# The triangular inverse of an RWKV block done in two halves of the heads instead of all at once

## The chip, the cores and the metric

The kernel runs on one core of a Trainium2 chip. The metric is the device time of one execution in microseconds (us), lower is better. The engines are PE (TensorE), DVE (VectorE), ACT (ScalarE), POOL (GpSimd) and SP (SyncE), which here only issues DMAs.

## The reference: two transformer blocks, the first of them with RWKV heads

The input is 512 tokens by 1024 channels in float32. The first block projects its normalised input once with `w_in`, and uses the columns for a dilated attention (three groups of heads), for an RWKV-7 time mix (8 heads of 64) and for gates. Then come an output projection, a squared-ReLU MLP and a gated embedding with `w_ple`. The second block has a differential attention, a pooling branch and another MLP; this change does not touch it.

```python
def rwkv7_time_mix(z, mu, w0, w2, a0, a2, g2, k_k, k_a, r_k, ln_w, ln_b):
...
    def step(state, inp):
        r_t, w_t, k_t, v_t, a_t, b_t = inp
        sa = jnp.einsum('bhvk,bhk->bhv', state, a_t)
        state = (state * w_t[:, :, None, :] + sa[..., None] * b_t[:, :, None, :]
                 + v_t[..., None] * k_t[:, :, None, :])
        y = jnp.einsum('bhvk,bhk->bhv', state, r_t)
        return state, y
...
def first_block(x, p, mix_pre_norm, w_in, ...):
        u = rmsnorm(h, mix_pre_norm[i])
        z = u @ w_in[i]
...
        o_attn = dilated_attention_branch(z_attn)
        o_rwkv = rwkv7_time_mix(z_rwkv, ...)
        gate_attn, gate_rwkv = jnp.split(jax.nn.sigmoid(z_gate), 2, axis=-1)
        merged = gate_attn * (o_attn @ w_attn_up[i]) + gate_rwkv * (o_rwkv @ w_rwkv_up[i])
        h = h + rmsnorm(merged @ w_out[i], mix_post_norm[i])
        f = rmsnorm(h, ffn_pre_norm[i])
        f = jnp.square(jax.nn.relu(f @ w_ff_in[i])) @ w_ff_out[i]
        h = h + rmsnorm(f, ffn_post_norm[i])
        e = (p[i] @ w_ple[i]) * jax.nn.sigmoid(h @ w_ple_gate[i])
        h = h + rmsnorm(e, ple_post_norm[i])
```

The recurrence is computed in chunks. Within a chunk the effect of `sa` on later tokens is a triangular system: for each head and each stretch of 32 tokens a unit triangular 32x32 matrix is inverted. With 8 heads and 16 stretches there are 128 such matrices, one for each partition of the memory.

## The kernel before: one queue of matmul chains, and lanes that are let in between

**Matmuls and their weights.** Products in float32 accuracy are made of float32r matmuls on split operands: each weight piece is loaded by a DMA of SP, ACT copies it to a rounded high part (`hi`), and `lo = raw - hi` is one subtraction on DVE or POOL. `fm_job` and `tm_job` are such chains over 1024 channels; a chain reads the pieces one after another, three matmuls to each 128 channels (high x high, low x high, high x low). Inside `vv(g)`, a `tm_job` of 256 columns makes the values of attention group g: four tiles of tokens, each a chain of 24 matmuls, from four pieces of weights.

**Lanes.** All else of the block (rope, attention streams, the RWKV work) sits in generators that are called lanes. `run`, `service` and `advance` step them while the chains are written out, with the help of a small planner that keeps a planned time for each engine. So the order on each engine is fixed when the program is built, and a change in one lane can move rows of others. `free` picks the engine of each subtraction in the same manner: POOL only where the planner holds it ahead of DVE by more than `BLOCK`. Every instruction is recorded at one helper line, L352, so rows are told apart by tiles. G is a tile of 128x512, Q one of 128x1024, `ps` a PSUM tile; `md`, `ud`, `vd` and `spill` lie in DRAM.

**The RWKV lanes.** `rwkv_prep` j (j = 0 to 3, a pair of heads each) ends by writing its matrices to `md` and setting `em[j]`. `rwkv_inverse` waits for all four events, loads the 128 diagonal blocks into CI (Q), and clears U (Q) on POOL. Then 31 steps follow, each of two DVE operations on U: a product into `tmp` (Q) and an addition into U, of (32-q)*q elements a partition, 31 at either end and 256 in the middle. Every second step the lane gives way to others. At the end ACT makes the transposed copy, eight DMAs write both to `ud`, two bring them back into `ub` in another layout, and `rwkv_feed` is started. It starts the units, four (c = 0 to 3) of the first two pairs and then four of the other two, at most two at a time. A unit loads its part M of `md` and does its 32x32 and 128x64 matmuls on PE. `rwkv_out` j follows the last unit of pair j, and sets `eo[j]`, which the `w_rwkv_up` chains need.

Of the kernel before, what the change touches and what calls it, by code (L numbers as in the profile page):

```python
# [14 lines left out]
ALU = mybir.AluOpType  # L15
# [3 lines left out]
P = 128  # L19
# [347 lines left out]
class Builder:  # L367
# [13 lines left out]
    UNITS = 2  # L381
    HEADS = 4
    BETWEEN = (0, 1, 1, 1, 1, 1, 0, 0)
    STEPS = 2
    SOON = 300.0
    MUST = 1
    ROOM = 12
# [41 lines left out]
    def swap_top(self):  # L429

        self.top.close()
        self.R = self.A = None
        self.pt = self.top.enter_context(self.tc.tile_pool(name="more", bufs=1, reuse_waits="tile"))
# [692 lines left out]
    def rwkv(self, u):  # L1126
        I = self.I
        w = I["w_in"][0]
        base = 2304
        R = self.R = {k: [None] * 4 for k in ("r", "k", "v", "ar", "bt", "kt", "n2", "bo", "em", "eo", "oh", "ol", "vc", "y")}  # L1130
        R["em"] = [Ev() for _ in range(4)]
        R["eo"] = [Ev() for _ in range(4)]
        R["einv"] = Ev()
        R["lora"] = Ev()
        R["exl"] = Ev()
        R["ez"] = {(k, j): Ev() for k in "rkv" for j in range(4)}
# [226 lines left out]
            self.sp.dma_start(out=t, in_=R["sp"][j, i])  # L1363

    def rwkv_inverse(self):
        R = self.R
        for j in range(4):
            yield R["em"][j], 3000
        CI, U, tmp = (self.q((P, 32, 32)) for _ in range(3))
        for b in range(4):  # L1370
            bs = slice(b * 32, b * 32 + 32)
            self.sp.dma_start(out=CI[bs], in_=R["md"][bs, :, bs].rearrange("s u t -> u s t"))
        self.pool.memset(U, 0.0)
        self.pool.memset(U.rearrange("p a b -> p (a b)")[:, 0:1024:33], 1.0)
        yield 0, 5000
        for q in range(31, 0, -1):
            tv = tmp[:, 0:q, 0:32 - q]
            self.dve.tensor_tensor(out=tv, in0=CI[:, 0:q, q:q + 1].to_broadcast([P, q, 32 - q]),
                                   in1=U[:, q:q + 1, q:32].to_broadcast([P, q, 32 - q]), op=ALU.mult)
            self.dve.tensor_tensor(out=U[:, 0:q, q:32], in0=U[:, 0:q, q:32], in1=tv, op=ALU.add)  # L1380
            if q % self.STEPS == 0:
                yield "dve", 800
        tmp = tv = None
        UT = CI
        self.act.copy(out=UT, in_=U.rearrange("p s t -> p t s"))
        yield 0, 1500
        R["ub"] = []
        for i, t in enumerate((U, UT)):
            for b in range(4):
                bs = slice(b * 32, b * 32 + 32)  # L1390
                self.sp.dma_start(out=R["ud"][i][bs].rearrange("s u t -> u s t"), in_=t[bs])
        U = UT = CI = t = None
        yield 0, 0
        for i in range(2):
            d = self.q((P, 32, 32))
            self.sp.dma_start(out=d, in_=R["ud"][i])
            R["ub"].append(d)
        yield 0, 7000
        self.set(R["einv"])
        R["S"] = {}  # L1400
        R["es"] = {(j, c): Ev() for j in range(4) for c in range(4)}
        R["ey"] = {(j, c): Ev() for j in range(4) for c in range(4)}
        self.spawn(self.rwkv_feed(), "feed")

    def rwkv_feed(self):

        R = self.R
        k = 0
        for j0 in (0, 2):
            for c in range(4):  # L1410
                while R["active"] >= self.UNITS or len(self.sg.free) < self.ROOM:
                    yield 0, 500
                if c == 0:
                    for j in (j0, j0 + 1):
                        if j >= 2:
                            self.reload(j)
                            yield 0, 0
                        R["vc"][j], R["y"][j] = self.g((P, 4, P)), self.g((P, 4, P))
                R["active"] += 1
                self.spawn(self.rwkv_unit(j0, c, k), f"unit{j0}{c}")  # L1420
                k += 1
# [1054 lines left out]
```

## Time and profile before

| what | us |
|---|---|
| runs | 1648.22, 1643.09, 1647.63 (median 1647.63) |
| the profiled execution's own time | 1644.16 |
| its span, first to last instruction | 1642.4 |
| PE busy in the span | 1620.8 |
| DVE, ACT, POOL busy | 1036.6, 671.0, 192.1 |
| the inverse's 62 DVE operations | 155.7 to 205.1, 23.8 busy |

The table's busy times are sums over the whole span. The profile's times count from the span's start. PE matmuls are pipelined and their ends modelled, so PE's idle time is what its waits show, and the granted clock of a stretch tells whether PE ran at its full rate there.

### The profile page before, as it was taken

The numbers are of one execution on the slowest core, as the hardware profiler recorded it, in microseconds if no ns is written. First come the engines' busy times: TensorE is split into PE (matmuls) and PEld (weight loads), VectorE is DVE, ScalarE is ACT, GpSimd is POOL, SyncE is SP. The second block draws the span as 40 slices with busy tenths as digits, with TensorE's granted clock in tenths as the row PEclk, the third lists the DMA queues.
The fourth block names the chain that finished last, engine by engine and source line by source line (L and its number), as shares of the span: only waits on it lengthen the run. The fifth ranks groups of instructions, "written<-read, shape, count | busy, mean of one in ns | idle before, by whom it ended". The sixth has DMA issues, their size and how long they took to land.

```text
span 1642.4 us, 24840 instructions
## 1 busy us (share of the span) xinstructions
PE 1620.8 (99%) x9249; PEld 1365.3 (83%) x9249; DVE 1036.6 (63%) x2157; ACT 671.0 (41%) x1486; POOL 192.1 (12%) x201
## 2 busy tenths in 40 slices
PE   9999999999999999999999999999999999999998
PEld 6888888788789988888899997777788888888888
DVE  5888954485666555444457767888866534444665
ACT  5644344333444453223256642333534442333332
POOL 3131100212001010000001030233110000000100
PEclk9999999999999999999999999999999999999999
DMA  8236352312552353333325331212333223333321
GB/s 241 68 97 187 97 129 77 98 39 84 161 166 65 93 132 111 88 90 100 98 65 148 91 97 52 65 55 74 91 103 103 75 80 103 99 89 101 103 77 52
DMA packets 289409, 161.95 MB, mean 99 GB/s; under 512 B 24612, under 2 KB 279208, under 8 KB 289288
## 3 DMA queue, kind: packets, MB, share of 16 engines
q1 hardware_dynamic: 289160, 160.24, 34.1%
q8 instruction: 72, 1.18, 0.3%
q0 software_dynamic: 128, 0.13, 0.1%
q14 instruction: 49, 0.40, 0.1%
HBM read 149.32 MB, written 11.01 MB: 98 GB/s over the span
## 4 chain that ended last, share of the span: by engine, by line
PE 87%; DVE 5%; issue 4%; ACT 2%; DMA 1%; SPq 1%; POOL 0%; POOLq 0%; DVEq 0%; ACTq 0%
PE ps L352 87%; DVE G L352 4%; ACT G L352 2%; SPq L352 1%; DMA G<-in_w_in_dram 1%; DVE s L352 0%; DMA cst<-in_consts_dram 0%; DMA G<-md 0%; POOL s L352 0%; DVE msk L352 0%; POOL G L352 0%; DVE Q L352 0%; POOLq L2472 0%; DVEq L2472 0%; ACTq L352 0%
## 5 line engine op out<-in xcount | busy, mean ns | idle before, releaser
L352 PE MATMUL ps<-G,G 128*128 128x512 f32 (+5 forms) x8248 | 1552.9, 353 | 9.7 <-ACT G L352 6.2
L352 PEld LDWEIGHTS ps<-G,G 128*128 128x128 f32 (+3 forms) x8248 | 1282.6, 187 | 246.9 <-issue 26.1
L352 DVE TENSOR_TENSOR G<-G,G 128x512 fp32r<-128x512 f32 (+3 forms) x881 | 533.8, 640 | 159.0 <-ACT G L352 145.3
L352 ACT CAST G<-G 128x512 fp32r<-128x512 f32 (+2 forms) x565 | 303.1, 589 | 46.4 <-DVE G L352 28.0
L352 DVE TENSOR_TENSOR G<-ps,G 128x512 f32<-128x512 f32 (+3 forms) x204 | 127.9, 631 | 125.6 <-PE ps L352 122.2
L352 ACT ACTIVATE G<-ps 128x512 f32<-128x512 f32 (+1 forms) x108 | 54.9, 516 | 321.5 <-PE ps L352 321.4
L352 ACT ACTIVATE G<-G 128x512 fp32r<-128x512 f32 (+4 forms) x210 | 110.3, 543 | 157.6 <-DVE G L352 153.4
L352 POOL TENSOR_TENSOR G<-G,G 128x512 f32<-128x512 f32 (+3 forms) x69 | 88.5, 1291 | 702.7 <-ACT G L352 594.8
L352 DVE SCALAR_TENSOR_TENSOR G<-ps,G 128x512 f32<-128x512 f32 (+1 forms) x70 | 44.7, 645 | 173.2 <-ACT G L352 173.2
L352 ACT COPY G<-ps 128x256 f32<-128x256 f32 (+5 forms) x172 | 63.5, 381 | 176.0 <-PE ps L352 163.0
L352 ACT ACTIVATE G<-G,s 128x256 f32<-128x256 f32 (+3 forms) x96 | 50.9, 531 | 111.4 <-DVE s L352 111.4
L352 POOL TENSOR_TENSOR s<-s,mhalf 128x2 f32<-128x2 f32 (+3 forms) x17 | 22.1, 1301 | 450.9 <-DVE s L352 450.9
L352 ACT ACTIVATE G<-G,vcol 128x256 f32<-128x256 f32 (+3 forms) x81 | 44.1, 545 | 43.3 <-DVE G L352 42.3
L352 PEld LDWEIGHTS ps<-cst,G 128*128 128x128 f32 x396 | 48.5, 158 | 10.9 <-DVE G L352 3.3
L352 PE MATMUL ps<-cst,G 128*128 128x128 f32 (+2 forms) x396 | 54.9, 263 | 1.1 <-DVE G L352 0.9
L352 DVE COPY G<-ps 128x128 f32<-128x128 f32 (+3 forms) x76 | 26.2, 353 | 35.8 <-PE ps L352 24.0
L352 DVE SCALAR_TENSOR_TENSOR G<-G,vcol,G 128x256 fp32r<-128x256 f32 (+4 forms) x57 | 34.0, 602 | 7.1 <-ACT G L352 7.1
L352 DVE SCALAR_TENSOR_TENSOR G<-G,G 128x512 fp32r<-128x512 f32 (+2 forms) x47 | 28.1, 606 | 6.4 <-ACT G L352 6.3
L352 DVE CUSTOM_DVE_ANT_0 G<-ps,mk 128x128 f32<-128x128 f32 (+3 forms) x64 | 28.6, 484 | 1.9 <-PE ps L352 1.9
L352 DVE CUSTOM_DVE_ANT_0 G<-G 128x128 f32<-128x128 f32 (+1 forms) x34 | 12.5, 374 | 25.1 <-ACT G L352 24.9
L352 POOL TENSOR_TENSOR G<-Q,cst 128x512 f32<-128x512 f32 (+1 forms) x16 | 15.6, 990 | 101.6 <-PE ps L352 79.0
L352 DVE TENSOR_TENSOR G<-ps,rb 128x512 f32<-128x512 f32 (+2 forms) x30 | 20.3, 684 | 10.8 <-PE ps L352 10.5
(121 smaller groups left out, 503.4 us busy)
## 6 DMA issues: line engine op xcount, KB each, us to landing
G<-in_w_in_dram SPq DMA_DIRECT2D x180, 256.0 KB, 3.6
G<-in_w_ff_in_dram SPq DMA_DIRECT2D x64, 256.0 KB, 3.0
G<-in_w_ff_out_dram SPq DMA_DIRECT2D x64, 256.0 KB, 3.2
G<-in_w_up_dram SPq DMA_DIRECT2D x64, 256.0 KB, 2.9
G<-in_w_down_dram SPq DMA_DIRECT2D x64, 256.0 KB, 3.3
G<-in_w_out_dram SPq DMA_DIRECT2D x32, 256.0 KB, 4.6
G<-in_w_ple_gate_dram SPq DMA_DIRECT2D x16, 256.0 KB, 3.7
spill<-G SPq DMA_DIRECT2D x10, 256.0 KB, 4.4
```

The costliest lines, as they stand in the source:

```text
L352: return f(*[u(x) for x in a], **{q: u(x) for q, x in k.items()})
```

## The change: two passes of 64 partitions, and the first units after the first pass

`rwkv_inverse` now makes two passes. Pass 0 waits for `em[0]` and `em[1]` and handles the blocks of the first two pairs, on partitions 0 to 63; then `rwkv_feed` starts. Pass 1 waits for `em[2]` and `em[3]` and does the rest, on partitions 64 to 127; the feed waits for `einv[1]` before it starts units of these pairs. Each pass has 62 DVE operations of the same lengths along a partition as the one pass had. The loads, clears, transposed copy, writes and loads back are made once a pass, on half the blocks, with 8 writes to `ud` in each pass. `tmp` is now half a G slot, so one Q tile fewer is used, and the tiles of `ub` are taken at the start. The lane gives way every third step.

```diff
--- before.py
+++ after.py
@@ -381,7 +381,7 @@
     UNITS = 2
     HEADS = 4
     BETWEEN = (0, 1, 1, 1, 1, 1, 0, 0)
-    STEPS = 2
+    STEPS = 3
     SOON = 300.0
     MUST = 1
     ROOM = 12
@@ -1130,7 +1130,7 @@
         R = self.R = {k: [None] * 4 for k in ("r", "k", "v", "ar", "bt", "kt", "n2", "bo", "em", "eo", "oh", "ol", "vc", "y")}
         R["em"] = [Ev() for _ in range(4)]
         R["eo"] = [Ev() for _ in range(4)]
-        R["einv"] = Ev()
+        R["einv"] = [Ev() for _ in range(2)]
         R["lora"] = Ev()
         R["exl"] = Ev()
         R["ez"] = {(k, j): Ev() for k in "rkv" for j in range(4)}
@@ -1363,50 +1363,55 @@
             self.sp.dma_start(out=t, in_=R["sp"][j, i])
 
     def rwkv_inverse(self):
+
         R = self.R
-        for j in range(4):
-            yield R["em"][j], 3000
-        CI, U, tmp = (self.q((P, 32, 32)) for _ in range(3))
-        for b in range(4):
-            bs = slice(b * 32, b * 32 + 32)
-            self.sp.dma_start(out=CI[bs], in_=R["md"][bs, :, bs].rearrange("s u t -> u s t"))
-        self.pool.memset(U, 0.0)
-        self.pool.memset(U.rearrange("p a b -> p (a b)")[:, 0:1024:33], 1.0)
-        yield 0, 5000
-        for q in range(31, 0, -1):
-            tv = tmp[:, 0:q, 0:32 - q]
-            self.dve.tensor_tensor(out=tv, in0=CI[:, 0:q, q:q + 1].to_broadcast([P, q, 32 - q]),
-                                   in1=U[:, q:q + 1, q:32].to_broadcast([P, q, 32 - q]), op=ALU.mult)
-            self.dve.tensor_tensor(out=U[:, 0:q, q:32], in0=U[:, 0:q, q:32], in1=tv, op=ALU.add)
-            if q % self.STEPS == 0:
-                yield "dve", 800
-        tmp = tv = None
-        UT = CI
-        self.act.copy(out=UT, in_=U.rearrange("p s t -> p t s"))
-        yield 0, 1500
-        R["ub"] = []
-        for i, t in enumerate((U, UT)):
-            for b in range(4):
-                bs = slice(b * 32, b * 32 + 32)
-                self.sp.dma_start(out=R["ud"][i][bs].rearrange("s u t -> u s t"), in_=t[bs])
-        U = UT = CI = t = None
-        yield 0, 0
-        for i in range(2):
-            d = self.q((P, 32, 32))
-            self.sp.dma_start(out=d, in_=R["ud"][i])
-            R["ub"].append(d)
-        yield 0, 7000
-        self.set(R["einv"])
         R["S"] = {}
         R["es"] = {(j, c): Ev() for j in range(4) for c in range(4)}
-        R["ey"] = {(j, c): Ev() for j in range(4) for c in range(4)}
-        self.spawn(self.rwkv_feed(), "feed")
+        R["ub"] = [None, None]
+        for j in range(2):
+            yield R["em"][j], 0
+        CI, U = (self.q((P, 32, 32)) for _ in range(2))
+        R["ub"] = [self.q((P, 32, 32)) for _ in range(2)]
+        for p in range(2):
+            for j in (2 * p, 2 * p + 1):
+                yield R["em"][j], 3000
+            ps, us = slice(64 * p, 64 * p + 64), slice(16 * p, 16 * p + 16)
+            blocks = [(slice(b * 32, b * 32 + 32), slice(64 * p + 16 * b, 64 * p + 16 * b + 16)) for b in range(4)]
+            tmp = self.w2((P, 256))
+            for bs, rs in blocks:
+                self.sp.dma_start(out=CI[rs], in_=R["md"][bs, us, bs].rearrange("s u t -> u s t"))
+            self.pool.memset(U[ps], 0.0)
+            self.pool.memset(U[ps].rearrange("p a b -> p (a b)")[:, 0:1024:33], 1.0)
+            yield 0, 5000
+            for q in range(31, 0, -1):
+                n = 32 - q
+                tv = tmp[ps, 0:q * n].rearrange("p (a b) -> p a b", a=q)
+                self.dve.tensor_tensor(out=tv, in0=CI[ps, 0:q, q:q + 1].to_broadcast([64, q, n]),
+                                       in1=U[ps, q:q + 1, q:32].to_broadcast([64, q, n]), op=ALU.mult)
+                self.dve.tensor_tensor(out=U[ps, 0:q, q:32], in0=U[ps, 0:q, q:32], in1=tv, op=ALU.add)
+                if q % self.STEPS == 0:
+                    yield "dve", 800
+            tmp = tv = None
+            self.act.copy(out=CI[ps], in_=U[ps].rearrange("p s t -> p t s"))
+            yield 0, 1500
+            for i, t in enumerate((U, CI)):
+                for bs, rs in blocks:
+                    self.sp.dma_start(out=R["ud"][i][bs, us].rearrange("s u t -> u s t"), in_=t[rs])
+            yield 0, 0
+            for i in range(2):
+                self.sp.dma_start(out=R["ub"][i][:, us], in_=R["ud"][i][:, us])
+            t = None
+            yield 0, 7000
+            self.set(R["einv"][p])
+            if p == 0:
+                self.spawn(self.rwkv_feed(), "feed")
 
     def rwkv_feed(self):
 
         R = self.R
         k = 0
         for j0 in (0, 2):
+            yield R["einv"][j0 // 2], 0
             for c in range(4):
                 while R["active"] >= self.UNITS or len(self.sg.free) < self.ROOM:
                     yield 0, 500
```

How this moves the program's rows is shown below at three places. Names carry the tile's kind, and two numbers that count allocations; they differ between the two programs.

DVE, before, around the values of the first attention group (`vv(0)`): `G_245` in the last row is the low part of that job's fourth piece; the rows ahead of it are rope (shuffle, products) and are followed by no row of the inverse for long.

```order
L352 TENSOR_TENSOR G_239_1258<-G_224_1141,G_223_1140 128x512
L352 TENSOR_TENSOR G_231_1183<-G_231_1183,G_203_1056 128x512
L352 STREAM_SHUFFLE G_240_1261<-ps_32_1176 128x512
L352 TENSOR_TENSOR G_241_1262<-ps_32_1176,G_202_1055 128x512
L352 TENSOR_TENSOR G_242_1277<-G_232_1184,G_231_1183 128x512
L352 TENSOR_TENSOR G_240_1261<-G_240_1261,G_203_1056 128x512
L352 TENSOR_TENSOR G_245_1289<-G_226_1164,G_244_1288 128x512
```

DVE, after, the same place: `G_244` is now that low part, `Q_6` is U and `G_204` is `tmp`.

```order
L352 TENSOR_TENSOR G_224_1155<-G_224_1155,G_203_1056 128x512
L352 STREAM_SHUFFLE G_240_1263<-ps_32_1191 128x512
L352 TENSOR_TENSOR G_241_1264<-ps_32_1191,G_202_1055 128x512
L352 TENSOR_TENSOR G_204_1077<-Q_5_1073,Q_6_1074 64x156
L352 TENSOR_TENSOR Q_6_1074<-Q_6_1074,G_204_1077 64x26x6
L352 TENSOR_TENSOR G_204_1077<-Q_5_1073,Q_6_1074 64x175
L352 TENSOR_TENSOR Q_6_1074<-Q_6_1074,G_204_1077 64x25x7
L352 TENSOR_TENSOR G_204_1077<-Q_5_1073,Q_6_1074 64x192
L352 TENSOR_TENSOR Q_6_1074<-Q_6_1074,G_204_1077 64x24x8
L352 TENSOR_TENSOR G_244_1295<-G_227_1179,G_243_1294 128x512
```

Sixteen operations of pass 0 now stand ahead of this low part (six of them shown), where none stood before. Of the other rows between the two programs' last common one on DVE and this one, two predicated copies and five 128x512 operations no longer stand there; four of the five are on POOL.

POOL, after, from the third to the fourth piece of the values of the second group (`vv(1)`): `G_282`, `G_300` and `G_315` are the low parts of that job's first, second and fourth piece.

```order
L352 TENSOR_TENSOR G_282_1566<-G_268_1503,G_281_1565 128x512
L352 TENSOR_SCALAR G_290_1623<-G_181_913,hb 128x2
L352 TENSOR_SCALAR G_291_1624<-G_181_913,hb 128x2
L352 TENSOR_TENSOR G_285_1593<-G_285_1593,G_203_1056 128x512
L352 TENSOR_TENSOR G_300_1690<-G_274_1551,G_299_1689 128x512
L352 TENSOR_TENSOR G_290_1623<-G_189_957,G_287_1616 128x2x128
L352 TENSOR_TENSOR G_291_1624<-G_189_957,G_287_1616 128x2x128
L352 TENSOR_SCALAR G_306_1718<-G_272_1543,hb 128x512
L352 MEMSET G_310_1726 128x512
L352 MEMSET G_311_1727 128x512
L352 TENSOR_TENSOR G_315_1766<-G_276_1555,G_314_1765 128x512
```

Before, all four low parts of this job stood on DVE, the fourth in this row, behind eight operations of the inverse:

```order
L352 TENSOR_TENSOR Q_7_1672<-Q_5_1670,Q_6_1671 128x28x4
L352 TENSOR_TENSOR Q_6_1671<-Q_6_1671,Q_7_1672 128x28x4
L352 TENSOR_TENSOR G_316_1748<-G_297_1644,G_315_1747 128x512
```

Three of the four are on POOL now; the third stays on DVE and has 46 operations of pass 0 ahead of it. Between these points POOL has eight more operations of 128x512 and two of 128x256 than before. In front of this job PE has 36 small matmuls fewer than before, those of the fourth pair's `rwkv_prep`, which now come later.

SP, after, at the end of pass 1 (`G_424` and `G_429` are the parts M of two units):

```order
L352 DMA G_417_2716<-in_w_in_dram 128x4x128
L352 DMA G_420_2721<-in_w_in_dram 128x4x128
L352 DMA G_424_2754<-md 128x4x128
L352 DMA ud_124<-Q_6_1074 16x32x32 x4
L352 DMA ud_125<-Q_5_1073 16x32x32 x4
L352 DMA G_429_2810<-md 128x4x128
L352 DMA Q_7_1075<-ud_124 128x512
L352 DMA Q_8_1076<-ud_125 128x512
```

SP, before, where the first two units' parts M are loaded:

```order
L352 DMA G_403_2428<-in_w_in_dram 128x4x128
L352 DMA G_404_2430<-in_w_in_dram 128x4x128
L352 DMA G_413_2450<-md 128x4x128
L352 DMA G_418_2486<-md 128x4x128
```

The load of the fourth unit's M now stands behind the eight writes of pass 1, which wait for its last DVE operation and the transposed copy. On PE, the first unit's rows begin 134 rows earlier than before, and `rwkv_out` of the last two pairs ends 36 rows earlier against the chains with `w_ple`; from row 2353, in the `w_out` stage, on, PE's order is the same. Both programs have 8012 rows on PE.

## Rows read from the trace of the kernel before

**Rows 1.** The page: busy time of PE, and the chain that ended last by engine.

```profile
PE 1620.8 (99%) x9249; PEld 1365.3 (83%) x9249; DVE 1036.6 (63%) x2157; ACT 671.0 (41%) x1486; POOL 192.1 (12%) x201
PE 87%; DVE 5%; issue 4%; ACT 2%; DMA 1%; SPq 1%; POOL 0%; POOLq 0%; DVEq 0%; ACTq 0%
```

**Rows 2.** Waits of PE over the whole span: total us, times, longest.

```profile
PE ps L352 <- ACT G L352: 6.2, 5, 2.9
PE ps L352 <- DVE G L352: 5.4, 7, 2.2
PE ps L352 <- POOL s L352: 2.0, 2, 1.3
PE ps L352 <- DMA G<-md: 1.1, 1, 1.1
```

**Rows 3.** Busy time by stretch: length, PE, PEld, DVE, ACT, POOL, clock, DMA.

```profile
99.10:169.80 70.70, 70.70 (x443) 60.19 (x442) 61.74 (x142) 30.88 (x85) 16.33 (x19) 1.00 0.51 145
205.30:260.00 54.70, 53.64 (x479) 46.66 (x478) 27.30 (x75) 24.29 (x66) 6.78 (x9) 0.97 0.45 111
220.00:240.00 20.00, 18.94 (x191) 15.29 (x192) 10.29 (x31) 6.21 (x19) 2.52 (x4) 0.91 0.41 110
320.00:340.00 20.00, 17.76 (x136) 13.47 (x136) 15.80 (x34) 7.07 (x15) 2.32 (x2) 0.91 0.15 39
420.00:440.00 20.00, 16.91 (x75) 13.43 (x74) 10.68 (x18) 10.92 (x20) 0.00 (x0) 1.00 0.22 74
```

**Rows 4.** Timeline of PE: start, us, operation, idle before it and its releaser.

```profile
229.31 0.44 PE L352 MATMUL ps<-Q,G 32*32 32x32 f32 x16 [1.06 <-DMA G<-md]
...
328.80 5.12 PE L352 MATMUL ps<-G,G 64*64 64x64 f32 x20 [2.24 <-DVE G L352]
...
430.58 0.50 PE L352 MATMUL ps<-G,G 128*128 128x512 f32 x1 [2.87 <-ACT G L352]
```

**Rows 5.** The inverse's operations as one group: busy, mean ns.

```profile
L352 DVE TENSOR_TENSOR Q<-Q,Q 128x31 f32<-128x31 f32 (+15 forms) x62 | 23.8, 384 | 1.6
```

**Rows 6.** Timeline of DVE, 155 to 182.

```profile
155.71 2.19 DVE L352 TENSOR_TENSOR Q<-Q,Q 128x31 f32<-128x31 f32 x8
157.81 0.69 DVE L352 TENSOR_TENSOR G<-G,G 128x512 fp32r<-128x512 f32 x1
158.41 1.35 DVE L352 TENSOR_TENSOR Q<-Q,Q 128x135 f32<-128x135 f32 x4
...
162.17 1.50 DVE L352 TENSOR_TENSOR Q<-Q,Q 128x175 f32<-128x175 f32 x4
...
179.31 2.67 DVE L352 TENSOR_TENSOR Q<-Q,Q 128x255 f32<-128x255 f32 x2
```

**Rows 7.** Timeline of DVE, 99 to 130.

```profile
100.70 2.85 DVE L352 TENSOR_TENSOR_SCAN G<-cst,G 128x128 f32<-128x128 f32 x4 [1.60 <-ACT G L352]
104.40 1.94 DVE L352 SCALAR_TENSOR_TENSOR G<-G,hb,G 128x254 f32<-128x254 f32 x2 [0.85 <-ACT G L352]
...
107.89 0.68 DVE L352 SCALAR_TENSOR_TENSOR G<-G,G 128x512 f32<-128x512 f32 x1
...
116.02 1.35 DVE L352 COPY_PREDICATED G<-cst,ps 128x512 f32<-128x512 int32 x2
...
119.69 3.15 DVE L352 TENSOR_TENSOR G<-G,G 128x512 f32<-128x512 f32 x6
...
127.56 1.43 DVE L352 TENSOR_TENSOR G<-G,G 128x256 fp32r<-128x256 f32 x4 [0.87 <-ACT G L352]
```

**Rows 8.** Timeline of POOL, 104 to 182.

```profile
104.45 1.61 POOL L352 TENSOR_TENSOR G<-G,G 128x256 f32<-128x256 f32 x2 [1.81 <-ACT G L352]
...
108.32 1.39 POOL L352 TENSOR_TENSOR G<-G,G 128x512 fp32r<-128x512 f32 x1
...
179.53 2.17 POOL L352 TENSOR_TENSOR G<-G,G 128x512 f32<-128x512 f32 x1 [11.33 <-issue]
```

**Rows 9.** PE's matmuls by form, 99.1 to 122: busy, mean ns.

```profile
L352 PE MATMUL ps<-cst,G 128*128 128x2 f32 x16 | 1.9, 240 | 0.0
L352 PE MATMUL ps<-G,G 128*128 128x256 f32 x11 | 1.5, 283 | 0.0
```

**Rows 10.** PE's matmuls by form, 163 to 166.

```profile
L352 PE MATMUL ps<-G,G 128*128 128x256 f32 x4 | 0.7, 307 | 0.0
```

**Rows 11.** PE's matmuls by form, 166 to 170.

```profile
L352 PE MATMUL ps<-G,G 128*128 128x256 f32 x35 | 4.4, 283 | 0.0
```

**Rows 12.** Timeline of SP's queue, 205 to 226: start, us in the queue.

```profile
205.35 6.38 SPq L352 DMA_DIRECT2D ud<-Q  x8
...
212.83 2.43 SPq L352 DMA_DIRECT2D Q<-ud  x2
...
224.08 1.54 SPq L352 DMA_DIRECT2D G<-md  x2
```

## The prediction

> **What bounds the kernel now.** I read the page's busy times first: PE is busy for 1620.8 of the 1642.4 us of the span, and 87% of the chain that ended last is PE's own work [rows 1]. Both programs have the same 8012 rows on PE, so the change can only add or remove waits of PE, and time at a lower clock behind them. Next come PE's waits: 14.7 us in all, in 15 pieces [rows 2]. Three of them belong to the RWKV part. At 229.31 a unit waits 1.06 us for its part M of `md`; at 328.80 another waits 2.24 us for DVE; at 430.58 a `w_ple` chain, whose products share the stretch with the last `rwkv_out`, waits 2.87 us for six casts on ACT [rows 4]. By stretches, the first two are followed by a lower clock: the mean granted clock is 0.91 in 220 to 240 and in 320 to 340, but 1.00 in 420 to 440 [rows 3]. A mean of 0.91 over 20 us is 3.6 us at the lower of the two levels (1.2 instead of 2.4 GHz), in which 1.8 us of work are lost. So the first two waits cost 1.06 + 2.24 + 2 x 1.8 = 6.9 us, the third 2.9. No PE row waits for the inverse itself: from 99.1 to 169.8 PE is busy in all of the 70.70 us, while DVE is busy in 61.74 and POOL in 16.33; from 205.3 to 260, with the first units, DVE is busy in only 27.30 of 54.70 [rows 3]. So the change moves DVE work out of a stretch with room for it, into one with little. There is no wait for `eo` to be won, since the `w_rwkv_up` chains come after the wait at 430.58.
>
> **The inverse's own cost.** The 62 operations take 23.8 us [rows 5]. The first 16 take 2.19 + 1.35 + 1.50 = 5.04 [rows 6], and the last 16, which have the same lengths in reverse, about as much. Half the partitions shorten no operation here, since the lengths along a partition are the same; no row of before shows this very operation on 64 partitions. I take the same price, so the two passes cost 23.8 us of DVE more than the one; were a half pass to cost half, nothing would be added (the bound below). What counts is where the steps stand.
>
> **Values of the first group.** PE comes to this job some 11 x 0.125 us before 122, at 120.6, and reads its fourth piece after 18 matmuls, at 122.9 (35 take 4.4 us) [rows 9, 11]. Its low part is the third of the six operations from 119.69, and so is there at about 121.3 [rows 7]: 1.6 us early. The change puts 16 operations of pass 0 ahead of it (5.0 us) and takes away two predicated copies (1.35) and five 128x512 operations (about 0.62 each, 3.1): DVE has 0.6 us more. POOL has four 128x512 operations more, 1.39 each [rows 8]: 5.6 us. If the two engines run side by side, 0.6 is under 1.6 and PE waits for nothing. If they take turns, it is 6.2 - 1.6 = 4.6 us.
>
> **Do they take turns?** At 179.31 two steps of the inverse take 2.67 us, where such steps take about 0.44 each, while POOL's 128x512 addition takes 2.17 instead of 1.39 [rows 6, 8]. So here they do, for operations that read two tiles of the main memory on both engines, and those are the ones added. The Trainium skill, "SBUF — State Buffer", "Who interferes with whom", has it as a lock: a DVE operation with two such inputs and a GpSimd operation that reads there exclude each other for a whole instruction. The trace agrees in that one overlap, with its 2.67 us; by the rule alone every added operation of POOL would be paid in full.
>
> **Values of the second group.** PE comes here at 166 - 4 x 0.125 = 165.5 [rows 10], reads the fourth piece 2.25 us later, at 167.7, and its low part is ready at 158.5 [rows 6]: 9.2 us early. PE's 36 moved matmuls, at some 0.10 us each (16 of one kind in 1.9 us [rows 9], others shorter), bring PE here 3.7 us sooner, so that 5.5 are left. DVE has 38 operations of the inverse more: 23.8 less the first eight (2.19) and the last 16 (5.0) is 16.6, or 14.8 without the one held at 179.31. It has less: twelve 128x512 operations (7.4), two 128x256 (0.7), two scalar-tensor operations (1.4), two predicated copies (1.35), and some small ones of `rwkv_prep` (2.0), in all 12.9 (by kinds as in [rows 7]): +1.9. POOL has eight 128x512 (11.1) and two 128x256 operations (0.81 each, 1.6) more [rows 8]: +12.7. Side by side, 1.9 is under 5.5 and nothing waits. In turn, 14.6 - 5.5 = 9.1 us, the first job's wait included, since a PE that waited there comes later here. Idle time of DVE in the stretch could take some of it: 70.70 - 61.74 = 9.0 us [rows 3], but the longest pieces are waits for ACT's results (1.60 and 0.85 [rows 7]), which a step can fill only if it happens to stand ahead. So the waits before the second job's end lie between 0 and 9.1; I take **7**, near the end that the overlap at 179.31 supports.
>
> **Units and pass 1.** The first units now run beside pass 1. Its 23.8 us fit into the 27.4 us that DVE had free in 205.3 to 260, but the units' short copies of PSUM stand between its operations. In before the eight writes of `ud` held SP's queue for 6.38 us and the two loads back for 2.43 [rows 12]. In after that happens twice; the load of the fourth unit's M, and weights, stand behind the second time. I take **+4** (0 if the work of other chains covers it; 6.4 + 2.4 = 8.8 if PE waits out one such train).
>
> **What goes.** The wait at 430.58: `rwkv_out` of the last pairs ends 36 PE rows earlier there, so ACT and DVE have less to do beside the six casts: **-2.9** (0 if the casts alone cause it). The waits at 229.31 and 328.80 belong to units that stand elsewhere now; the same loads and copies exist in the same order, so I take half, **-3.4** (0 to -6.9). New waits of 2 us and more can lower the clock as those two did; the one of 2.87 did not: **+1.8**, one such stretch (0 to 5.4).
>
> **The sum.** 7 + 4 - 2.9 - 3.4 + 1.8 = +6.5 us. On the profiled execution's 1644.16 this is 1650.7; that execution lies 3.5 under the median of the runs, 1647.63, so the forecast for the median is **1654**. A measurement here tells about 0.3%, 4.9 us, from no change (under 1642.7 is faster, over 1652.5 slower).
>
> **Rivals.** *Faster:* the units begin earlier and their own waits disappear: -6.9 and -2.9, no new lower clock, the value jobs wait 3 and the units nothing: -6.8, about 1641. For it speaks that the three waits lie in RWKV work, and that DVE is half idle where pass 1 goes; against it, that a load of M takes some 5 us (queued from 224.08, awaited until 229.31 [rows 4, 12]) on a queue that is now more often blocked. It decides if the waits at the value jobs stay under 5 us. *The change doesn't do anything that PE sees:* the value jobs wait some 2 us, the units change one wait for another, the wait at 430.58 goes: -1 to +3, about 1649. The full PE of 99 to 170 speaks for it, and so does half the price for half the partitions, if that is so. *Much slower:* taking turns is paid in full, 9.1, with pass 1 in the way of units and SP, 8.8, and two or three stretches of lower clock, 4.5; against -2.9: some +19, about 1667.
>
> **Chances.** Forecast (+2 to +11) 0.50, no effect 0.22, faster 0.18, much slower 0.10. Of the forecast's 0.50 some 0.10 lie below +4.9. So slower has 0.50, within 0.3% 0.33, faster 0.17. The range takes in the faster rival's upper part and most of the slower one's: 1643 to 1664. The likeliest case alone is 1650 to 1659.
>
> **What would show it.** In the profile after: PE's matmuls of 128x256 for the two value jobs should have idle time before them, released by POOL or DVE; POOL's 128x512 operations in 99 to 170 should take 2 us or more, and steps of the inverse beside them over 1 us; the 124 half operations should cost about 47 us. The wait of 2.87 at a `w_ple` chain should be gone. I am wrong if PE is full up to the second value job, if half operations cost half, or if the clock is 1.00 in all stretches with units.

## The result and the profile after: seven microseconds slower, and PE waits at the two value jobs

The changed kernel takes 1654.64 us (median of 5 runs, 1654.15 to 1655.27) against 1647.63 (1643.09 to 1648.92): a ratio of 1.0051, with a 95% interval of 1.0038 to 1.0065. On another chip, in one of the experiments, the ratio was 1.0036 (1.0023 to 1.0049). By these two ratios the loss is 6 to 8 us. The profiled execution of after took 1654.57 us, with a span of 1652.8; that span is 10.4 us longer than the one of before, whose profiled execution was a quick one.

The page of after, PE's line and the granted clock by slices (answers to [rows 1]):

```profile
PE 1625.8 (98%) x9249; PEld 1369.0 (83%) x9249; DVE 1059.0 (64%) x2210; ACT 673.6 (41%) x1487; POOL 202.6 (12%) x212
...
PEclk9999899999999999999999999999999999999999
```

PE's busy time has risen by 5.0 us with the same instructions, and the fifth slice (165 to 207 us) has a lower clock. The view of PE's waits (as [rows 2]: total, times, longest):

```profile
PE ps L352 <- DVE G L352: 7.8, 12, 1.6
PE ps L352 <- DVE mxA L352: 6.3, 1, 6.3
PE ps L352 <- ACT G L352: 3.1, 4, 1.3
PE ps L352 <- POOL s L352: 2.0, 2, 1.3
PE ps L352 <- DVE msk L352: 0.2, 1, 0.2
```

The wait for `md` is gone, ACT's longest has fallen from 2.9 to 1.3, and a wait of 6.3 us is new. PE's timeline, the rows that begin after a wait of over 0.5 us between 100 and 400 (as [rows 4]):

```profile
124.53 25.91 PE L352 MATMUL ps<-G,G 128*128 128x256 f32 x152 [1.65 <-DVE G L352]
...
171.54 7.18 PE L352 MATMUL ps<-G,G 128*128 128x256 f32 x36 [6.31 <-DVE mxA L352]
...
220.57 8.29 PE L352 MATMUL ps<-G,G 64*128 64x256 f32 x46 [1.25 <-DVE G L352]
...
258.73 0.66 PE L352 MATMUL ps<-cst,G 128*128 128x128 f32 x4 [0.88 <-DVE G L352]
```

The first two rows are the values of the first and of the second group. The other two belong to units. The waits at 229.31, 328.80 and 430.58 of before have no successor here. By hundreds of us:

```profile
100.00:200.00 100.00, 92.04 (x566) 79.05 (x564) 86.93 (x202) 39.38 (x107) 27.20 (x28) 0.95 0.40 112
200.00:300.00 100.00, 97.14 (x839) 82.16 (x838) 70.81 (x192) 38.71 (x105) 14.80 (x16) 0.98 0.42 108
300.00:400.00 100.00, 99.20 (x810) 80.97 (x807) 66.30 (x135) 36.11 (x95) 20.32 (x19) 1.00 0.28 76
400.00:500.00 100.00, 97.81 (x497) 81.18 (x497) 64.65 (x101) 43.53 (x84) 7.16 (x5) 1.00 0.51 153
```

In before the same four stretches had 100.00, 98.94, 97.76 and 95.36 us of busy PE: the first stretch has lost 8.0 us, and the last won 2.5.

**What PE waits for at 171.54.** DVE's timeline ahead of it, and two rows of POOL's:

```profile
163.24 1.67 DVE L352 TENSOR_TENSOR G<-G,G 128x512 f32<-128x512 f32 x2
164.81 0.34 DVE L352 TENSOR_TENSOR G<-Q,Q 64x192 f32<-64x192 f32 x1
165.19 2.17 DVE L352 TENSOR_TENSOR Q<-Q,G 64x192 f32<-64x192 f32 x1
167.39 0.33 DVE L352 TENSOR_TENSOR G<-Q,Q 64x175 f32<-64x175 f32 x1
167.76 0.33 DVE L352 TENSOR_TENSOR Q<-Q,G 64x175 f32<-64x175 f32 x1
168.13 0.31 DVE L352 TENSOR_TENSOR G<-Q,Q 64x156 f32<-64x156 f32 x1
168.47 0.31 DVE L352 TENSOR_TENSOR Q<-Q,G 64x156 f32<-64x156 f32 x1
168.71 2.08 DVE L352 TENSOR_TENSOR G<-G,G 128x256 fp32r<-128x256 f32 x6
170.72 0.41 DVE L352 CUSTOM_DVE_ANT_0 G<-ps,cst 128x256 f32<-128x256 f32 x1
171.06 0.08 DVE L352 DVE_READ_ACCUMULATOR2_ANT mxA<- 128x1 f32 x1
171.06 0.41 DVE L352 CUSTOM_DVE_ANT_0 G<-ps,cst 128x256 f32<-128x256 f32 x1
```

```profile
157.13 1.33 POOL L352 TENSOR_TENSOR G<-G,G 128x512 fp32r<-128x512 f32 x1
165.05 2.10 POOL L352 TENSOR_TENSOR G<-G,G 128x512 f32<-128x512 f32 x1 [6.59 <-DVE G L352]
```

The last low part of the second value job, on POOL, is there at 157.13 + 1.33 = 158.5, and PE does the job's first chain without a wait. The second chain writes to PSUM buffer `ps0`, where the scores of an attention lane lie. With the buffers' numbers, the program's order shows it (PE's row of the scores, PE's first row of the second chain, and DVE's last read of the scores; the number after the engine counts its rows):

```
PE  693  MATMUL ps0_52_1757<-G63_259_1419,G27_254_1351 128x256
PE  728  MATMUL ps0_58_1864<-G39_281_1565,G15_16_163 128x256
DVE 227  ISA G65_325_1806,mxA_126<-ps0_52_1757,cst_74 128x256
```

That read ends at 171.06 + 0.41 = 171.47, and PE goes on at 171.54. Ahead of it DVE has six operations of pass 0 from 164.81 to 168.78 (3.97 us), one of them held for 2.17 us while POOL's addition at 165.05 runs, and then six low parts of later weights, whose work PE does not need yet.

**The clock behind it.** Stretches of 2 us:

```profile
166.00:168.00 2.00, 0.00 (x0) 0.00 (x0) 1.93 (x3) 0.00 (x0) 1.94 (x2) 0.81 0.00 0
168.00:170.00 2.00, 0.00 (x0) 0.00 (x0) 1.93 (x7) 0.00 (x0) 0.30 (x2) 0.50 0.00 0
...
176.00:178.00 2.00, 2.00 (x13) 2.00 (x13) 1.63 (x6) 0.70 (x2) 0.00 (x0) 0.63 0.00 0
178.00:180.00 2.00, 2.00 (x21) 2.00 (x20) 0.37 (x1) 2.00 (x2) 0.00 (x0) 1.00 0.37 131
```

PE is idle from 165.2 to 171.5. The granted clock falls to 0.50, the lower of the two levels (1.2 GHz), at 167.2, and rises again at 177.5 (from the means 0.81 and 0.63 of the two stretches at the edges). So 5.9 us of work (171.5 to 177.5) run at half speed, and 3.0 us are lost beyond the wait.

### The profile page after: what moved, and what is told of

Its sections match the earlier page's. It is cut to its first block, busy times and chain, and to the rows that moved or that the text cites. A ratio compares the mean times of both kernels' runs of the same rounds, so it can differ in the third digit from the quotient of the medians.

```text
span 1652.8 us, 24920 instructions
## 1 busy us (share of the span) xinstructions
PE 1625.8 (98%) x9249; PEld 1369.0 (83%) x9249; DVE 1059.0 (64%) x2210; ACT 673.6 (41%) x1487; POOL 202.6 (12%) x212
## 4 chain that ended last, share of the span: by engine, by line
PE 77%; DVE 8%; issue 4%; ACT 1%; POOL 0%; DMA 0%; DVEq 0%; POOLq 0%; ACTq 0%
PE ps L352 77%; DVE G L352 7%; ACT G L352 1%; DVE Q L352 1%; DVE s L352 0%; POOL s L352 0%; DMA G<-in_w_ple_dram 0%; POOL G L352 0%; ACT Q L352 0%; POOLq L2477 0%; DVEq L2477 0%; DVE msk L352 0%; ACTq L352 0%; DVEq L352 0%; DVE ss L352 0%
## 5 line engine op out<-in xcount | busy, mean ns | idle before, releaser
L352 PE MATMUL ps<-G,G 128*128 128x512 f32 (+7 forms) x8248 | 1557.3, 353 | 14.9 <-DVE mxA L352 6.3
L352 PEld LDWEIGHTS ps<-G,G 128*128 128x128 f32 (+4 forms) x8248 | 1287.4, 187 | 254.4 <-issue 24.5
L352 DVE TENSOR_TENSOR G<-G,G 128x512 fp32r<-128x512 f32 (+3 forms) x872 | 526.6, 638 | 150.6 <-ACT G L352 134.6
L352 POOL TENSOR_TENSOR G<-G,G 128x512 fp32r<-128x512 f32 (+3 forms) x78 | 99.7, 1287 | 731.0 <-ACT G L352 613.0
L352 DVE TENSOR_TENSOR Q<-Q,G 64x31 f32<-64x31 f32 (+16 forms) x66 | 29.1, 442 | 2.2
L352 DVE TENSOR_TENSOR G<-Q,Q 64x31 f32<-64x31 f32 (+16 forms) x64 | 26.9, 420 | 1.7
```

The lines of the kernel that those rows point to most:

```text
L352: return f(*[u(x) for x in a], **{q: u(x) for q, x in k.items()})
```

## The experiments: steps left out, an engine exchanged, passes moved, turns made longer

Times are medians; ratios are to the kernel before, run on the same chip among the others, with 95% intervals.

**The changed kernel again**, unedited.

> The changed kernel once more, on the same chip as the next three and the kernel before: 3 to 8 us over before, PE's waits at 124 and 171 as in its first profile, 1.7 and 6.3 us.

1654.12 us, 1.0036 (1.0023 to 1.0049), waits of 1.63 and 5.92 us. It gives the base of the next ratios.

**Pass 0 without its operations.** The planner still counts them, so every other instruction keeps its place:

```diff
+                dve = (lambda **k: self.plan.op("dve", "tensor_tensor", (), k)) if p == 0 else self.dve.tensor_tensor
-                self.dve.tensor_tensor(out=tv, in0=CI[ps, 0:q, q:q + 1].to_broadcast([64, q, n]),
+                dve(out=tv, in0=CI[ps, 0:q, q:q + 1].to_broadcast([64, q, n]),
...
-                self.dve.tensor_tensor(out=U[ps, 0:q, q:32], in0=U[ps, 0:q, q:32], in1=tv, op=ALU.add)
+                dve(out=U[ps, 0:q, q:32], in0=U[ps, 0:q, q:32], in1=tv, op=ALU.add)
```

> The changed kernel, every instruction at its place, with the 62 DVE operations of pass 0 left out (the planner still counts them, so the order stays; the first two pairs use the unit matrix as inverse). Theory A (pass 0's operations stand ahead of DVE work that PE needs at the two value jobs): the waits of 1.65 and 6.31 us at 124 and 171 and the lower clock behind the second (some 2.9 us) go, so the time falls from 1654.6 to 1643 to 1646. Theory B (the loss lies in the units, their DMAs and pass 1): the time stays at 1652 to 1655.

1645.57 us, 0.9976 (0.9964 to 0.9987): by the ratios 10 to 12 us less than the changed kernel (1.0036 and 1.0051), and both waits and the lower clock between 100 and 200 are gone (PE busy for 99.86 of 100 us). That is about what the two waits and the clock behind them add up to, 1.65 + 6.31 + 3.0 = 11.0 us; the units' waits of 1.25 and 0.89 us stay. Theory A holds.

**Pass 1 without its operations**, in the same way (`p == 1`).

> The changed kernel with the same order and the 62 DVE operations of pass 1 left out instead. Theory A: only the units' waits beside pass 1 can go (1.25 and 0.88 us and, with the first, 1.7 us of lower clock), so 1651 to 1654. Theory B: most of the loss of 7 us goes, 1646 to 1649.

1652.92 us, 1.0017 (1.0007 to 1.0027), so 3 to 6 us less by ratios, 1.6 less by the spans of the profiles. The waits at 124 and 171 stay (2.51 and 5.91 us here); the units' waits of 1.25 and 0.88 go:

```profile
200.00:300.00 100.00, 99.78 (x884) 84.97 (x883) 49.24 (x135) 40.95 (x111) 16.21 (x17) 1.00 0.46 127
```

Pass 1 beside the units costs less than pass 0, but not nothing.

**POOL's work on DVE.** During pass 0, `free` hands out DVE where it chose POOL; the order is the same.

```diff
+        self.asdve = Eng(tc.nc.vector, "pool", self.plan)
...
-        return self.pool if max(self.plan.t["pool"], t) + 200 + 2.1 * n + self.BLOCK < d else self.dve
+        pool = self.asdve if self.nopool else self.pool
+        return pool if max(self.plan.t["pool"], t) + 200 + 2.1 * n + self.BLOCK < d else self.dve
```

> The changed kernel with the same order, but the twelve tensor operations that POOL does for weights and rope during pass 0 issued on DVE. DVE gets some 7 us more of its own. Theory A with taking turns (POOL's 1.3 us each hold DVE off): DVE loses 7 us and gains back up to 13, so the waits at the value jobs become shorter, 1649 to 1654. Rival (the engines run side by side and only DVE's own sum counts): the waits grow by 5 to 7 us, 1659 to 1662.

1653.28 us, 1.0025 (1.0014 to 1.0037): 2 to 4 us less by the ratios, although DVE has twelve operations more. The first wait is gone, the second is 4.60 us. The same six steps of the inverse in its DVE timeline:

```profile
162.88 0.35 DVE L352 TENSOR_TENSOR G<-Q,Q 64x192 f32<-64x192 f32 x1
163.26 0.35 DVE L352 TENSOR_TENSOR Q<-Q,G 64x192 f32<-64x192 f32 x1
163.65 0.33 DVE L352 TENSOR_TENSOR G<-Q,Q 64x175 f32<-64x175 f32 x1
164.02 0.33 DVE L352 TENSOR_TENSOR Q<-Q,G 64x175 f32<-64x175 f32 x1
164.38 0.31 DVE L352 TENSOR_TENSOR G<-Q,Q 64x156 f32<-64x156 f32 x1
164.73 0.31 DVE L352 TENSOR_TENSOR Q<-Q,G 64x156 f32<-64x156 f32 x1
164.97 2.69 DVE L352 TENSOR_TENSOR G<-G,G 128x512 fp32r<-128x512 f32 x7
```

They take 2.1 us here, and 3.97 in after, where POOL adds meanwhile. So the engines do take turns, and what POOL had taken over from DVE gained nothing here. Here PE waits for the low part of the job's fourth piece, the first of the seven operations at 164.97.

**Six operations out of 62.** As for pass 0 above, but only for `q in (6, 7, 8)`: those at 164.81 to 168.78.

> The changed kernel with only six operations of pass 0 left out, those of q = 8, 7, 6, which stand on DVE right ahead of six low parts of weights and the reads of the attention scores whose PSUM buffer the second chain of the second value job takes over (four us in the changed kernel's profile, 1.8 of them held while POOL adds). If DVE's queue ahead of these reads sets the wait of 5.9 to 6.3 us at 171, the wait falls to 2 to 3, with less of the lower clock behind it, and the time by 4 to 7 us to 1647 to 1650. If the wait is for the fourth piece's low part on POOL, as the prediction had it, it stays at 6 and the time at 1653 to 1655.

1650.16 us, 1.0009 (1.0000 to 1.0019), by the ratios 4 to 7 us less. PE's waits at the two value jobs:

```profile
124.81 25.91 PE L352 MATMUL ps<-G,G 128*128 128x256 f32 x152 [1.50 <-DVE G L352]
...
167.55 6.07 PE L352 MATMUL ps<-G,G 128*128 128x256 f32 x36 [2.04 <-DVE mxA L352]
```

The second wait is 2.04 us, where the changed kernel's two profiles have 5.92 and 6.31. It is shorter by the 4 us that the six took, and the first has stayed. What PE waits for is DVE's queue ahead of the reads of the scores; POOL's low part is not it.

**Both passes late.** The first pass waits for all four events, as the one pass did:

```diff
-        for j in range(2):
+        for j in range(4):
             yield R["em"][j], 0
         CI, U = (self.q((P, 32, 32)) for _ in range(2))
```

> Two passes, but the first waits for all four events as the one pass did; the feed still starts after pass 0. Theory A: no wait of PE at the value jobs, 1645 to 1650, and the units' part costs or gives what it does by itself. Theory B: the two trains of DMAs and the units beside pass 1 still cost, 1653 to 1656.

1655.31 us, 1.0038 (1.0026 to 1.0049). Theory A's 1645 to 1650 was wrong here and theory B's 1653 to 1656 right, though A's mechanism held: PE is busy for all of 100 to 200, but units wait later (the two longest):

```profile
248.15 1.91 PE L352 MATMUL ps<-G,G 64*128 64x256 f32 x10 [1.93 <-DVE G L352]
...
346.49 0.23 PE L352 MATMUL ps<-G,G 32*32 32x32 f32 x1 [3.03 <-ACT G L352]
```

and the wait at 430 is back (PE is busy for 16.86 of 20 us in 420 to 440). So the place of pass 0 is not the whole price of a second pass. The number of steps in a turn was still open, since the change had raised it from two to three. `STEPS` alone was set in the next ones.

**Two late passes by two and by six**, and **one pass by three, four and six** (the kernel before with only this number changed).

> Two passes after all four events, giving way every second step as the one pass did, instead of every third. If the loss of the late passes (1655 against 1650) comes from the groups of three steps, the time falls to 1648 to 1651; if it comes from the second pass beside the units and its second train of DMAs, it stays at 1653 to 1656.

> Two passes after all four events, giving way every sixth step. At the same number of steps it differs from the one pass by six (1636) by the split alone. If the split is neutral once pass 0 stands late (as by two: 1646 against 1648.5), it is at 1635 to 1639; if pass 1 beside the units costs, waits of PE at units appear between 230 and 330 and the time is 1643 to 1650.

> The kernel before with the change's other edit alone: one pass, giving way every third step instead of every second. If a coarser turn by itself helps as with six (1636), this lies between, 1640 to 1646; if what an order of instructions happens to do for the units decides, it may lie on either side of before by up to 5 us.

> The kernel before, giving way every fourth step. A trend from two (1648.5) to six (1636) would put it at 1640 to 1645, with the inverse ended 3 to 6 us earlier than in before and the waits at 229 or 430 gone.

> The kernel before, giving way every sixth step: the one pass is over sooner, and each turn holds DVE for up to 5 us. If an earlier end of the units is worth something by itself (the waits at 229, 328 and 430), this is faster than before, 1641 to 1647, with no wait of PE in 99 to 170. If longer turns of the inverse hold off what PE needs, as theory A says of pass 0, waits appear in 150 to 210 and the time is 1650 to 1656.

| steps in a turn | one pass | two late passes |
|---|---|---|
| 2 | 1 (the kernel before) | 1646.22 us, 0.9991 (0.9978 to 1.0004) |
| 3 | 1645.65 us, 0.9989 (0.9976 to 1.0001) | 1655.31 us, 1.0038 (1.0026 to 1.0049) |
| 4 | 1639.22 us, 0.9948 (0.9930 to 0.9967) | |
| 6 | 1636.29 us, 0.9927 (0.9910 to 0.9943) | 1647.63 us, 1.0005 (0.9994 to 1.0016) |

Three steps alone change nothing that is clear of noise, so this part of the change does not explain the loss by itself. By four and by six, longer turns help the one pass, by more than was expected of either, and against the guess that they would hold off what PE needs. Two late passes by two are also quicker than either case expected. In the one pass by six, PE has one wait of over half a us between 100 and 460 (the one behind it, in the `w_out` stage, is in all kernels), the inverse ends 8 us sooner (196.9 instead of 205.1), and the clock stays at 1.00 in all four stretches:

```profile
318.48 0.60 PE L352 MATMUL ps<-cst,mxB 128*4 128x128 f32 x4 [1.70 <-DVE G L352]
335.34 0.66 PE L352 MATMUL ps<-cst,G 128*128 128x128 f32 x4 [0.16 <-DVE G L352]
```

```profile
L352 DVE TENSOR_TENSOR Q<-Q,Q x62: 191/361/1384, 155.3 to 196.9; 128x31 f32<-128x31 f32 x4, 128x60 f32<-128x60 f32 x4, 128x87 f32<-128x87 f32 x4, 128x112 f32<-128x112 f32 x4
```

```profile
100.00:200.00 100.00, 100.00 (x616) 85.03 (x615) 89.47 (x219) 41.20 (x116) 24.27 (x25) 1.00 0.46 129
200.00:300.00 100.00, 100.00 (x910) 85.86 (x910) 50.86 (x138) 41.91 (x117) 9.65 (x13) 1.00 0.42 110
300.00:400.00 100.00, 98.14 (x794) 80.00 (x794) 63.80 (x129) 35.30 (x92) 22.85 (x22) 1.00 0.26 67
400.00:500.00 100.00, 98.44 (x551) 85.52 (x550) 63.31 (x103) 43.39 (x86) 9.41 (x8) 1.00 0.48 141
```

Gone are the waits of before at 229, 328 and 430 with the two stretches of lower clock (9.8 us by the prediction's rows); new is the one of 1.70. That is 8.1 us less, where the spans of the two profiles differ by 8.6 (1642.4 and 1633.8). The medians differ by 12 us, and the executions of this version have a mean clock of 0.998 or 0.999, so lower clock in other executions of before is likely the rest; no row shows it. This version beats both kernels. By the ratios the second pass costs 13 us at six steps and 8 at three; at two it costs nothing that can be measured. Two late passes by six have PE busy for less in 200 to 300, where pass 1 stands beside the units, than one pass by six has (100.00):

```profile
200.00:300.00 100.00, 94.98 (x811) 81.50 (x811) 72.46 (x185) 38.27 (x101) 11.51 (x12) 0.98 0.37 89
```

**The kernel before without its 62 operations**, with the same order.

> The kernel before, every instruction at its place, with the 62 DVE operations of its one pass left out (unit matrices in place of the inverses). Theory A: they were hidden beside the full PE, so the time stays within 3 us of before. Rival: they cost PE time there too (by the lock with POOL, or by later units): 4 us or more faster.

1644.47 us, 0.9971 (0.9961 to 0.9981): 4 us faster by the medians, 3 to 6 by the interval, so the rival holds, if narrowly. In its profile PE is busy for all of 220 to 240 at clock 1.00, so the wait at 229.31 is gone; the waits of 2.24 and 2.9 us are as in before. So the one pass was not wholly hidden either. Why the unit's load of M is in time once DVE has these 24 us less was not tried.

## Why the prediction was right: the value jobs, and one wait that was another

The forecast was 1654, the median 1654.64. By its own terms:

- **Value jobs, +7.** Measured 1.65 + 6.31 = 8.0 us, within the 0 to 9.1. The first wait has the mechanism but not the size: 4.6 us were priced if the engines take turns, and 1.65 were waited. The low part of the fourth piece, the first of the operations in this row of DVE, ends at about 124.5 and releases PE at 124.53:

```profile
123.80 2.69 DVE L352 TENSOR_TENSOR G<-G,G 128x512 fp32r<-128x512 f32 x7
```

  That is 3.2 us later than the 121.3 of before, where 6.2 were counted. For the second wait, the step that failed is "reads the fourth piece 2.25 us later", taken as what would be late. That low part came from POOL in time; late were DVE's reads of the scores, in whose PSUM buffer the job's second chain goes. The sum came out because it counted DVE's queue in that stretch, and the reads stand in the same queue.
- **Taking turns.** Held: steps of the inverse that ran beside an addition of POOL took about as long as it, 1.27, 1.17 and 1.35 us beside additions of 1.3, and 2.17 beside 2.10, where such steps take 0.3 to 0.4 otherwise. Exchanging engines took 1.9 us off the six steps. The sign that POOL's additions should take 2 us or more came true for that one alone. The Trainium skill, "SBUF — State Buffer", "Who interferes with whom", has a DVE instruction with two inputs in the main memory contend with a GpSimd instruction that reads there, over a port pair that is locked exclusively; these durations agree.
- **Same price on half the partitions.** Held: operations of 240 elements take 396 and 400 ns on 64 partitions, and 408 on 128. The 124 half operations took about 52 us, where 47 were forecast; steps held by POOL are in the 52.
- **Units and pass 1, +4.** PE's waits from 200 to 320 sum to 0.34 + 1.25 + 0.88 + 0.27 + 0.42 + 0.24 = 3.4 us (the first is a weight chain's). The term was too small all the same, since not all of the cost stands in waits. PE's busy time rose by 5.0 us, and lower clock explains only 1.1 of it (4.7 us of work lost, by the next item, against 3.6 in before). The remaining 3.9 point to the units' small matmuls. Their two forms, before and then after, at the same counts:

```profile
L352 PE MATMUL ps<-G,G 64*128 64x128 f32 x168 | 14.6, 283 | 0.0
L352 PE MATMUL ps<-G,G 64*128 64x256 f32 x88 | 14.0, 401 | 0.0
...
L352 PE MATMUL ps<-G,G 64*128 64x128 f32 x168 | 17.2, 285 | 0.0
L352 PE MATMUL ps<-G,G 64*128 64x256 f32 x88 | 16.6, 406 | 1.8 <-DVE G L352 1.5 <-DVE msk L352 0.2
```

  One of them takes no longer than before, but they are busy for 5.2 us more, of which other forms give some back: they follow one another more slowly, in gaps that the modelled ends of matmuls cover. The changed kernel's second profile has the same 17.2 and 16.6; without pass 1's operations they are 16.2 and 15.4, so a part comes from pass 1, and what holds up the rest isn't shown. With them the term is some 7.3, within its 0 to 8.8. Its reason was only half right: no wait for `md` is left and none is put down to a DMA, so SP's second train of writes shows no cost; what PE is seen to wait for is DVE.
- **What goes, -2.9 and -3.4.** The wait at 430.58 is gone. Of the two at 229 and 328, with their lower clock, I took half of 6.9; both went. Against it stands more lower clock than the +1.8 I took: 3.0 behind the wait at 171, and some 1.7 in 220 to 240 (at 0.91). The two errors cancel: -3.4 + 1.8 = -1.6 forecast, -6.9 + 4.7 = -2.2 measured.

By rows: 8.0 + 7.3 - 2.9 - 2.2 = +10.2, and the spans of the two profiles differ by 10.4. The forecast, worked out from the profile of before, was +6.5, so it missed 4 us, the part of the units that no wait shows. That it met the median is in part luck: the profiled execution of before lies 3.5 us under the median of its runs, while that of after (1654.57) lies at the median of its own, so the medians differ by only 7.0.

What the change set out from, units that begin sooner, did pay: the three old waits cost 9.8 us with their clock and are gone. They were paid for with 8.0 + 7.3 us and 4.7 of clock (the faster rival needed under 5 at the value jobs), since pass 0 went where DVE had 9 us to spare in 70, at the price of a whole pass.

What stays open: why a second pass costs nothing at two steps a turn and 13 us at six, and what slows the units' matmuls. Each number also moves other lanes, and no experiment held these fixed.

## What to carry to other kernels

A halved job costs half only along the axis that the engine's time runs on; here half the partitions cost as much as all, and the second half was a whole pass more. Before work is moved forward, count in the new place every reader behind it in the same queue: weights, but also reads that give PSUM back. Compare PE's busy time as well as its waits: some 4 us of the loss stood in no wait. When a lane's start is what is late, try first to let it finish sooner where it stands (longer turns: 12 us here) before it is split.

## What the runs showed beyond that

The spread of the kernel before goes with the clock: among 29 executions on one chip, those with a mean granted clock of 0.997 took 1644.1 to 1645.9 us, those with 0.992 took 1651.8 to 1653.2; a difference of 0.005 is 8 us of 1650. The four timed executions of one pass by six, at 0.998 and 0.999, lie within 1.5 us (1635.53 to 1637.03). The profiled execution of before (0.997) is one of its quickest.

The length of a wait alone does not tell whether the clock falls behind it. The one of 2.87 us at 430 in before did not lower it (1.00 in 430 to 450), while two late passes by three have 0.91 there, around a wait of 2.92. In the changed kernel itself the first value job's wait of 1.65 us is followed by a clock of 1.00 in 120 to 140, and in its second profile the same wait, of 1.63, by 0.91.
